# Sink columns copied ahead of the bias transfer, and padded value copies one step later, in a windowed-attention stage

## The chip, the cores and the metric

The kernel runs on one core of one Trainium2 chip. Its time is device microseconds (us) of one execution; lower is better. Five engines work from queues of their own, each strictly in the order in which the program lists its instructions: PE (TensorE: matrix products, with PEld for its weight loads), DVE (VectorE), ACT (ScalarE), POOL (GpSimd) and SP (SyncE, which here only issues DMA transfers). An instruction that waits for another engine or for a transfer holds everything behind it on its engine.

## What is computed

One step of a two-layer encoder for 1024 prompt frames and 32 sample frames, 1056 columns in all, at width 1024. Layer 0 is an mLSTM mixer with a feed-forward block. Layer 1 is attention in a sliding window with a feed-forward block, and only that attention is touched by the change. All heads use one shared pair of keys and values; each query sees its own chunk of 64 frames and the two chunks before it; a distance bias is added, and each head has a learned "sink", a score that takes part in the maximum and in the sum but has no value row:

```
s  = einsum('bcqhgd,bckhd->bchgqk', q, k) * HEAD_DIM ** -0.5 + bias
sk = sinks.reshape(N_KV_HEADS, GROUP)[:, :, None, None]
mx = maximum(max(s, -1), sk)
p  = exp(s - mx)
p  = p / (sum(p, -1) + exp(sk - mx))
o  = einsum('bchgqk,bckhd->bcqhgd', p, v)
x  = layer_norm(alpha * x + o @ w_out)
```

16 query heads share 2 key and value heads of size 64.

## The kernel before

All dense products run on PE as three matmuls for one (high times high, high times low, low times high), since operands are split in a rounded high part and a rest. A weight unit (`wr`, 512 KB) is loaded by SP at line 168, cast to its high part `wh` by ACT or POOL (lines 243 and 245), and the rest `wl` is formed by POOL or DVE (line 247). The helper `gemm` at lines 416 to 418 issues the matmuls and after each triple calls `wv.tick`, which moves a hand-written clock of "model microseconds" forward; generators launched on that clock (`wv.launch`) emit their instructions when their pause has run out. So the order in each queue is fixed when the program is written: dense matmuls with pieces of attention woven in between.

The frames are processed in three column groups (0 to 383, 384 to 767, 768 to 1055), and attention in nine tiles b: eight of 128 prompt frames, and b = 8 for the sample. Four pairs of query tiles `jp`, each of two tiles j, run over group 0 first, then over groups 1 and 2. A "visit" is one `jp` over the tiles of group 0, or over those of groups 1 and 2; the item (j, b) is one query tile on one frame tile. An item goes through these steps of `attention`:

- `scores`: PE forms the products into `psS` (line 1830); DVE adds bias and sink and takes the minimum in one instruction (line 1836, `s<-psS,bt`). At the first item of a visit, the bias of a coming visit is loaded by `load_bias`.
- `soft`: ACT takes exponentials (line 1851).
- `scale`: DVE takes reciprocals (line 1861), POOL multiplies (line 1864; for the first tile b = 0 and for the sample DVE does it, line 1868).
- `turn`: PE transposes the weights into a bank `T` (line 1889), ACT and DVE split them in `hi` and `lo` (lines 1893 and 1894).
- `values`: for odd j, PE multiplies with the values `VR` or with the padded values `VZ` into `O` (line 1918). It is emitted for tile b only once `ast["v"] > b`.
- `place`: ACT and DVE write the result to `act` (lines 1932 and 1936).

The bias tile `bt` holds two rows of 194 columns for each partition: 192 columns of distance bias from a DMA transfer (line 1720, issued by SP), and a sink column at each end of a row, written by two POOL copies (line 1724). There are three buffers of it, and nine loads: two at the start, and one at each of the visits 0 to 6. The sample's tile `sb` has its sink column at one end only (lines 1729 and 1732), one buffer and four loads.

The value tiles come from `v_turn`: for every tile c PE transposes a part of `vT` (line 1785), and `v_parts` splits it into `VR` with ACT and DVE (lines 1712 and 1713). Then `pad_values` copies one half of the partitions of tile c into one or two places of `VZ`, a POOL cast (line 1775). Three generators do this, for groups 0, 1 and 2, launched with pauses of 1.5, 5.0 and 2.5 model us, and 0.8 between tiles; group 0's also clears `VZ` (line 1781). `attention` begins 4.0 model us after its launch. Just before it, `k_spread` issues its DMA transfers of keys on SP (lines 1655 to 1659).

Of the kernel before, what the change touches and what calls it, by code (L numbers as in the profile page):

```python
# [30 lines left out]
WK = 3 * LC  # L31
# [259 lines left out]
def kernel(ctx: ExitStack, tc: tile.TileContext, A, O):  # L291
    nc = tc.nc
# [13 lines left out]
    def new(p, tag, shape, dt=F32, bufs=1):  # L306
        uid[0] += 1
        return p.tile(list(shape), dt, name=f"{tag}_{uid[0]}", tag=tag, bufs=bufs)
# [20 lines left out]
    for j in range(PAIRS):  # L329
        U_Q.append(add("wqk", 2 * j))  # L330
        U_K.append(add("wqk", 2 * j + 1))
        v = ("wv", 2 * j - 2) if j else ("wvg", 0)
# [1376 lines left out]
    def v_parts(c, src, L):  # L1709

        src = src.rearrange("p (g d) -> p g d", g=2)
        nc.scalar.copy(VR[:L, c, :, 0, :], src)
        nc.vector.tensor_sub(VR[:L, c, :, 1, :], src, VR[:L, c, :, 0, :].bitcast(F32))
# [3 lines left out]
    def load_bias(jp):  # L1717

        bt = B[jp] = new(pb, "bt", [P, 2, WK + 2], bufs=3)
        nc.sync.dma_start(bt[:, :, 1 : WK + 1], A["bias"][:, 2 * jp : 2 * jp + 2, :])  # L1720
        for h in range(2):
            r = slice(64 * h, 64 * h + 64)
            sink = nsink[r, 4 * jp + h : 4 * jp + 4 : 2]
            nc.gpsimd.tensor_copy(bt[r, :, 0 : WK + 2 : WK + 1], sink.unsqueeze(2).broadcast_to([64, 2, 2]))

    def load_sample_bias(jp):

        sb = SB[jp] = new(pb, "sb", [2 * DEC, 2, P + DEC + 1])
        nc.sync.dma_start(sb[:, :, 1:], A["sbias"][:, 2 * jp : 2 * jp + 2, :])
        for h in range(2):  # L1730
            r = slice(DEC * h, DEC * h + DEC)
            nc.gpsimd.tensor_copy(sb[r, :, 0], nsink[r, 4 * jp + h : 4 * jp + 4 : 2])

    load_bias(0)
    load_bias(1)
    load_sample_bias(0)
    def keys_values(g):
        if g == 2:
# [33 lines left out]
    def pad_values(i, c, g2):  # L1772

        r = slice(64 * i, 64 * i + 64)
        nc.gpsimd.tensor_copy(VZ[i][r, c - 1 + i], VR[r, c, g2].rearrange("p a d -> p (a d)").bitcast(F32))

    def v_turn(group, pause):
        yield pause
        if not group:
            for i in range(2):  # L1780
                nc.gpsimd.memset(VZ[i][64 * (1 - i) : 64 * (2 - i)].bitcast(F32), 0.0)
        for c, c0, L, g, off in CH:
            if g == group:
                pt = new(psb, "T", [P, 512], bufs=2)
                nc.tensor.transpose(pt[:L, :P], vT[g][:, off : off + L], ident[:])
                v_parts(c, pt[:L, :P], L)
                for i in range(2):
                    if 1 - i <= c < 8 - i:
                        pad_values(i, c, 0)
                ast["v"] = c + 1  # L1790
                yield 0.8

    ast = {"ready": 0, "scored": 0, "placed": 0, "v": 0, "visit": -1}

# [6 lines left out]
    def attention(gap):  # L1801
# [11 lines left out]
        def scores(j, b):  # L1813
            _, t0, R, g, off = CH[b]
            jp = j // 2
            if j % 2 == 0 and b in (0, 3):
                ast["visit"] += 1
                if ast["visit"] < 7:
                    load_bias((ast["visit"] + 1) % 4)
            s = S[j, b] = {}  # L1820
            q, g2, ps = Q[j, g], j // 4, psS[j % 2]
            bias = SB[jp] if b == 8 else B[jp]
            p = s["p"] = new(pb2, "s", [P, 2 * WK + 4], bufs=5)
            st = s["st"] = new(pb2, "st", [P, 3, 2], bufs=6)
            n = DEC if b == 8 else LC
            rows = 2 * n
            for c, at, _, nk, k0, _ in parts(b):
                lhs = q[:, 2 * (off + n * c) : 2 * (off + n * c) + rows]
                for i, k in enumerate((KH[g2], KL[g2])):
                    nc.tensor.matmul(ps[:rows, at : at + nk], lhs, k[:, k0 : k0 + nk], start=i == 0, stop=i == 1)  # L1830
            for c, src, at, nk, _, w in parts(b):
                first = b != 0 and c == 0
                cols = slice(at - first, at + nk + (not first))
                sc = slice(src - first, src + nk + (not first))
                bc = slice(w - first, w + nk + (not first))
                nc.vector.tensor_tensor_reduce(
                    p[:rows, cols], ps[:rows, sc], bias[:rows, j % 2, bc], 1.0, 3e38,
                    op0=ALU.add, op1=ALU.min, accum_out=st[:rows, 0, c : c + 1],
                )
            if b == 8 and j % 2 and jp < 3:  # L1840
                load_sample_bias(jp + 1)
            ast["scored"] += 1
# [111 lines left out]
    for t in spread:  # L1954
        wv.drain(t)
    wv.launch(v_turn(0, 1.5))
    wv.launch(v_turn(1, 5.0))
    task = wv.launch(attention(GAP_A))
    ast["ready"] = 4
    keys_values(2)  # L1960
    wv.launch(v_turn(2, 2.5))
    for t in spread:
        wv.drain(t)
# [182 lines left out]
```

## Time and profile before

| | |
|---|---|
| median of 3 runs | 2208.6 us (2207.87 to 2209.03) |
| the profiled execution, its own time | 2208.45 us |
| its span in the profile | 2206.7 us |
| mean granted TensorE clock | 0.995 of full speed |
| busy DVE, ACT, POOL | 1447.5, 986.7, 976.6 us |
| HBM traffic over the span | 129 GB/s |

Times within the span are counted from its start. The attention items run from about 1210 to 1421 us. A row of the timeline gives start, duration, engine, line, operation, what is written and read and with what shape, and in brackets how long the engine stood idle before it and who let it go. A row of the waits gives the total, the number of times and the longest. A row of the windows gives the length of the stretch, the busy time of each engine with its number of instructions, then PEclk (the granted TensorE clock, 1.00 is full speed), the DMA share and GB/s.

### The profile page before, as it was taken

The page shows a single profiled execution, that of the slowest core. Times are in us where ns is not written, and L with a number is a line of the kernel's source. Part 1 is how long each engine was busy: PE and PEld are TensorE (multiplying, and loading weights), DVE is VectorE, ACT ScalarE, POOL GpSimd, SP SyncE. Part 2 cuts the span into 40 slices and gives each one's busy share as a digit, 9 for nine tenths or more (in the row PEclk, how much of TensorE's full clock was granted, in tenths as well). Part 3 has the DMA queues.
Part 4 walks back from the last instruction along what each step waited for, and adds up shares of the span by engine and source line. Part 5 has one row for each costly group of instructions (what it writes and reads, how often), then busy time and mean ns, then how long its engine had stood idle before and what let it go on. Part 6 is the DMA issues. An engine that isn't in the chain of part 4 may idle for free.

```text
span 2206.7 us, 43768 instructions
## 1 busy us (share of the span) xinstructions
PE 2169.5 (98%) x16982; PEld 2141.5 (97%) x16982; DVE 1447.5 (66%) x2822; ACT 986.7 (45%) x2224; POOL 976.6 (44%) x987
## 2 busy tenths in 40 slices
PE   9999999999999999999999899999999999999997
PEld 9999999999999999999999889899999999999997
DVE  4465576787656655566668777788666666466657
ACT  4443455465444444322235676756444444332125
POOL 2544310004655555544526656600666555554441
PEclk9999999999999999999999999999999999999999
DMA  5221212212443343697515221411344434397712
GB/s 170 78 62 57 58 40 87 89 39 79 156 151 137 142 156 137 234 333 231 180 65 147 87 73 55 133 62 40 119 155 156 146 132 152 137 345 252 246 57 80
DMA packets 166192, 289.97 MB, mean 131 GB/s; under 512 B 16416, under 2 KB 121944, under 8 KB 165984
## 3 DMA queue, kind: packets, MB, share of 16 engines
q1 hardware_dynamic: 161632, 282.84, 38.4%
q10 hardware_dynamic: 4352, 4.33, 0.6%
q8 instruction: 134, 2.20, 0.4%
q14 instruction: 74, 0.61, 0.1%
HBM read 202.35 MB, written 82.94 MB: 129 GB/s over the span
## 4 chain that ended last, share of the span: by engine, by line
PE 84%; DVE 7%; ACT 4%; DMA 3%; issue 2%; POOL 0%; SPq 0%; ACTq 0%; DVEq 0%; POOLq 0%
PE d L416 10%; PE d L418 10%; PE d L417 10%; PE A L416 9%; PE A L417 9%; PE A L418 9%; PE B L416 7%; PE B L417 7%; PE B L418 7%; DMA sx<-hs_t 1%; PE O L1918 1%; ACT act L519 1%; PE psS L1830 1%; DMA sx<-hs_x 1%; PE T L1889 1%
## 5 line engine op out<-in xcount | busy, mean ns | idle before, releaser
L247 POOL TENSOR_TENSOR wl_s<-wr,wh_s 128x512 fp32r<-128x512 f32 x224 | 304.1, 1366 | 237.1 <-ACT wh_s L245 163.6
L416 PE MATMUL d<-sx,wh 128*128 128x264 f32 (+2 forms) x1040 | 333.2, 320 | 1.2 <-DVE act L1680 1.2
L247 POOL TENSOR_TENSOR wl_a<-wr,wh_a 128x512 fp32r<-128x512 f32 x112 | 153.2, 1370 | 402.0 <-ACT wh_a L245 397.5
L418 PE MATMUL d<-sx,wl 128*128 128x264 f32 (+2 forms) x1040 | 317.3, 305 | 1.0 <-POOL wl L247 1.0
L417 PE MATMUL d<-sx,wh 128*128 128x264 f32 (+2 forms) x1040 | 317.3, 305 | 1.1 <-DVE sx L531 1.1
L416 PE MATMUL A<-sx,wh_s 128*128 128x264 f32 x896 | 254.5, 284 | 0.0
L417 PE MATMUL A<-sx,wh_s 128*128 128x264 f32 x896 | 254.2, 284 | 0.0
L418 PE MATMUL A<-sx,wl_s 128*128 128x264 f32 x896 | 254.0, 283 | 0.0
L245 ACT CAST wh_s<-wr 128x512 fp32r<-128x512 f32 x224 | 135.7, 617 | 192.1 <-DVE wr L197 102.4
L416 PEld LDWEIGHTS d<-sx,wh 128*128 128x128 f32 x1040 | 197.3, 190 | 4.4 <-DVE act L1680 1.4
L417 PEld LDWEIGHTS d<-sx,wh 128*128 128x128 f32 x1040 | 197.5, 190 | 2.5 <-DVE sx L531 1.3
L418 PEld LDWEIGHTS d<-sx,wl 128*128 128x128 f32 x1040 | 196.8, 189 | 1.8 <-POOL wl L247 1.5
L416 PE MATMUL d<-sx,ex 128*128 128x264 f32 x624 | 180.7, 290 | 0.1
L418 PE MATMUL d<-sx,ex 128*128 128x264 f32 x624 | 177.0, 284 | 0.7 <-DVE ex L247 0.7
L417 PE MATMUL d<-sx,ex 128*128 128x264 f32 x624 | 177.2, 284 | 0.0
L418 PEld LDWEIGHTS A<-sx,wl_s 128*128 128x128 f32 x896 | 168.8, 188 | 0.0
L416 PEld LDWEIGHTS A<-sx,wh_s 128*128 128x128 f32 x896 | 168.4, 188 | 0.1
L417 PEld LDWEIGHTS A<-sx,wh_s 128*128 128x128 f32 x896 | 168.4, 188 | 0.0
L1346 POOL TENSOR_TENSOR z<-z 128x528 fp32r<-128x528 f32 x76 | 103.2, 1358 | 127.8 <-ACT z L1345 114.4
L247 POOL TENSOR_TENSOR wl<-wr,wh 128x512 fp32r<-128x512 f32 (+2 forms) x84 | 109.6, 1309 | 74.6 <-ACT wh L245 71.9
L416 PE MATMUL A<-ex,wh_s 128*128 128x264 f32 x448 | 127.5, 285 | 0.0
L417 PE MATMUL A<-ex,wh_s 128*128 128x264 f32 x448 | 127.1, 284 | 0.0
(378 smaller groups left out, 7211.2 us busy)
## 6 DMA issues: line engine op xcount, KB each, us to landing
wr<-in_gu SPq DMA_DIRECT2D x92, 512.0 KB, 4.6
hs_x<-z SPq DMA_DIRECT2D x72, 528.0 KB, 3.0
hs_t<-z SPq DMA_DIRECT2D x64, 528.0 KB, 2.8
sx<-hs_x SPq DMA_DIRECT2D x112, 264.0 KB, 5.9
sx<-hs_t SPq DMA_DIRECT2D x64, 264.0 KB, 6.4
ex<-hs_t SPq DMA_DIRECT2D x64, 264.0 KB, 6.7
wr<-in_dn SPq DMA_DIRECT2D x32, 512.0 KB, 3.9
ex<-hs_x SPq DMA_DIRECT2D x32, 264.0 KB, 5.0
```

The costliest lines, as they stand in the source:

```text
L245: self.nc.scalar.copy(hi, r)
L247: eng.tensor_sub(lo, r, hi.bitcast(F32))
L416: nc.tensor.matmul(out, ah, bh, start=start and k == 0, stop=False, **kw)
L417: nc.tensor.matmul(out, ah, bl, start=False, stop=False, **kw)
L418: nc.tensor.matmul(out, al, bh, start=False, stop=stop and k == last, **kw)
L519: nc.scalar.activation(z, z, AF.Identity, scale=gk, bias=bk)
L1346: eng.tensor_sub(lo.bitcast(F32R), buf(s), hi)
L1830: nc.tensor.matmul(ps[:rows, at : at + nk], lhs, k[:, k0 : k0 + nk], start=i == 0, stop=i == 1)
L1889: nc.tensor.transpose(pt[:nk, t, :rows], p[:rows, at : at + nk], ident[:rows, :rows])
L1918: nc.tensor.matmul(out, v[:nk], x, start=i == 0, stop=i == len(todo) - 1)
```

## The change

In `load_bias` and `load_sample_bias` the POOL copies of the sinks stand ahead of the DMA that brings the bias. In `v_turn` the padded copies of tile c are no longer emitted with that tile but two pauses later, just ahead of the transpose of tile c + 2; a last one follows 1.2 model us after the second-last. `ast["v"]`, the count of value tiles that are made, moves with them.

```diff
     def load_bias(jp):
         bt = B[jp] = new(pb, "bt", [P, 2, WK + 2], bufs=3)
-        nc.sync.dma_start(bt[:, :, 1 : WK + 1], A["bias"][:, 2 * jp : 2 * jp + 2, :])
         for h in range(2):
             r = slice(64 * h, 64 * h + 64)
             sink = nsink[r, 4 * jp + h : 4 * jp + 4 : 2]
             nc.gpsimd.tensor_copy(bt[r, :, 0 : WK + 2 : WK + 1], sink.unsqueeze(2).broadcast_to([64, 2, 2]))
+        nc.sync.dma_start(bt[:, :, 1 : WK + 1], A["bias"][:, 2 * jp : 2 * jp + 2, :])
 
     def load_sample_bias(jp):
         sb = SB[jp] = new(pb, "sb", [2 * DEC, 2, P + DEC + 1])
-        nc.sync.dma_start(sb[:, :, 1:], A["sbias"][:, 2 * jp : 2 * jp + 2, :])
         for h in range(2):
             r = slice(DEC * h, DEC * h + DEC)
             nc.gpsimd.tensor_copy(sb[r, :, 0], nsink[r, 4 * jp + h : 4 * jp + 4 : 2])
+        nc.sync.dma_start(sb[:, :, 1:], A["sbias"][:, 2 * jp : 2 * jp + 2, :])
...
     def v_turn(group, pause):
+        def pad(c):
+            for i in range(2):
+                if 1 - i <= c < 8 - i:
+                    pad_values(i, c, 0)
+            ast["v"] = c + 1
+
+        ready = []
         yield pause
...
                 v_parts(c, pt[:L, :P], L)
-                for i in range(2):
-                    if 1 - i <= c < 8 - i:
-                        pad_values(i, c, 0)
-                ast["v"] = c + 1
                 yield 0.8
+                if ready:
+                    pad(ready.pop())
+                ready.append(c)
+        yield 1.2
+        pad(ready.pop())
```

## The prediction

> **What bounds the kernel now.** I read the busy line of the page first, then PE's waits, then the POOL queue around the longest of them, then the chain of waits through it, and last the windows for the clock.
>
> ```profile
> span 2206.7 us, 43768 instructions
> PE 2169.5 (98%) x16982; PEld 2141.5 (97%) x16982; DVE 1447.5 (66%) x2822; ACT 986.7 (45%) x2224; POOL 976.6 (44%) x987
> ...
> PE T L1889 <- POOL s L1864: 6.3, 2, 5.1
> PE O L1918 <- DVE act L1936: 3.9, 4, 2.3
> ...
> POOL bt L1724 <- DMA bt<-in_bias: 25.4, 7, 8.9
> POOL VZ L1775 <- DVE VR L1713: 7.1, 1, 7.1
> ```
>
> PE sets the end: it stands idle for 2206.7 - 2169.5 = 37.2 us of the span. Shortening DVE, ACT or POOL is worth only what it takes from those 37.2 us or from stretches in which PE runs at a lower clock. The largest single wait, 5.1 us, is for a POOL multiplication (the `scale` step). POOL itself waits 25.4 us in seven places for bias transfers before it may copy the sinks. The question is how much of 25.4 lies under 5.1.
>
> ```profile
> 1211.43 0.62 POOL L1775 CAST VZ<-VR 64x128 fp32r<-64x128 f32 x2
> 1220.91 0.41 POOL L1724 COPY bt<-nsink 64x4 f32<-64x4 f32 x2 [8.86 <-DMA bt<-in_bias]
> 1221.39 0.61 POOL L243 CAST wh<-wr 128x512 fp32r<-128x512 f32 x1
> 1222.08 1.26 POOL L247 TENSOR_TENSOR wl<-wr,wh 128x512 fp32r<-128x512 f32 x1
> 1223.28 1.28 POOL L1775 CAST VZ<-VR 64x128 fp32r<-64x128 f32 x4
> 1224.64 0.82 POOL L1864 TENSOR_TENSOR s<-s,st 128x384 f32<-128x384 f32 x1
> ...
> 1225.52 0.90 PE L1889 MATMUL T<-ident,s 128*128 128x128 f32 x3 [5.05 <-POOL s L1864]
> ...
> 1216.36 0.15 DVE L1861 RECIPROCAL st<-st 128x2 f32<-128x2 f32 x1
> ...
> 1217.71 0.59 SPq L1720 DMA_DIRECT2D bt<-in_bias  x1
> ...
> 1212.05 8.84 issue
> ```
>
> POOL is done at 1212.05 and then stands until 1220.91, since SP reached this bias only at 1217.71 and it landed about 3.2 us later. Behind the copies stood a weight split, four padded copies and the multiplication that PE wanted. Its last input was the reciprocal of 1216.36. The chain of waits shows the same hole as 8.84 us of "issue". So PE's 5.05 us are a queueing effect: the multiplication was ready at 1216.5 and ran at 1224.64.
>
> ```profile
> 1220.50:1225.50 5.00, 0.00 (x0) 0.00 (x0) 0.45 (x4) 0.30 (x2) 4.19 (x10) 0.68 0.20 50
> 1225.50:1229.30 3.80, 3.78 (x15) 3.36 (x15) 1.34 (x7) 1.47 (x6) 3.60 (x6) 0.52 0.05 5
> 1229.30:1235.00 5.70, 5.70 (x40) 5.49 (x40) 3.84 (x14) 4.12 (x14) 2.66 (x6) 1.00 0.38 126
> 1430.00:2206.70 776.70, 762.81 (x6232) 759.57 (x6230) 510.94 (x700) 316.30 (x565) 337.89 (x256) 0.99 0.44 149
> ```
>
> The wait has a second price. For 3.80 us after it PE is busy, but at a granted clock of 0.52, so (1 - 0.52) x 3.80 = 1.82 us of work are lost. The last row shows why a gain here lasts: after 1430 PE is busy 762.81 of 776.70 us, so nothing later holds the end in place.
>
> **The sinks.** Nothing is added or removed: 18 copies for `bt`, 8 for `sb`, and 13 transfers all stay. Only the order of two queues against each other changes. POOL no longer waits for a transfer; SP's bias transfer waits for the copies instead, if the two are held to overlap, as the 25.4 us say that they are. At 1212.05 POOL goes on with copies 0.41, cast 0.61, split 1.26 and, were the padded copies still here, 1.28: done by about 1215.7. Then it waits for the reciprocal and multiplies from 1216.5 to 1217.3.
>
> ```profile
> 1220.13 0.34 PE L418 MATMUL d<-sx,wl 128*128 128x384 f32 x1
> ...
> 1221.36 0.23 DVE L1836 CUSTOM_DVE_ANT_0 s<-psS,bt 128x65 f32<-128x65 f32 x1 [1.04 <-POOL bt L1724]
> ...
> 1216.49 0.33 PE L1785 MATMUL T<-ident,act 128*128 128x128 f32 x1 [0.41 <-DVE VR L1713]
> 1218.58 0.38 PE L1889 MATMUL T<-ident,s 128*64 128x128 f32 x2 [0.79 <-DVE lo L1894]
> ```
>
> PE comes to this transpose at 1220.13 + 0.34 = 1220.47. The margin is 3.1 us, so the whole 5.05 us should go, and with it the slow clock, 1.82 us.
>
> What is late next is DVE's first use of this bias. It already waited to 1221.36 and now waits for the landing alone. Its split of PE's transposed tile stands behind that, so DVE reaches it at about 1221.8; PE has its second bank and a `values` product ready until then. In the 8.5 us before the stall PE lost 0.41 + 0.79 us to DVE; in the 5.7 us after it, none (5.70 of 5.70). I charge half of the 1.2 us, **0.6 us**, for a resumed stage with no pause in which DVE catches up.
>
> ```profile
> 1169.95 1.17 POOL L1724 COPY bt<-nsink 64x4 f32<-64x4 f32 x4 [4.17 <-DMA bt<-in_bias]
> ...
> 1205.21 0.40 PE L417 MATMUL d<-sx,wh 128*128 128x288 f32 x1 [1.05 <-DVE sx L531]
> 1207.42 0.40 PE L416 MATMUL d<-sx,wh 128*128 128x288 f32 x1 [1.17 <-DVE act L1680]
> 1208.50 0.36 PE L1785 MATMUL T<-ident,act 128*128 128x128 f32 x1 [0.42 <-DVE VR L1713]
> ...
> 1208.51 0.95 POOL L1775 CAST VZ<-VR 64x128 fp32r<-64x128 f32 x3 [7.14 <-DVE VR L1713]
> ```
>
> At the other six places nobody on PE waits for POOL's copies, so those waits vanish at a gain of nothing. One of them, 4.17 us, stands ahead of the stage. What POOL then does earlier meets DVE's normalisation work earlier. Bounds: PE's gaps at 1205 to 1208.5, 1.05, 1.17 and 0.42 us, are all behind DVE, so a gain of up to 2.64 us; a loss of 1 us if DVE is held at a worse moment. I take nothing: POOL's work changes its place, not its amount.
>
> **SP behind the copies.** SP now stands still until POOL has copied, and everything queued on SP stands with it. The longest new hold is at the seventh load:
>
> ```profile
> 1274.97 0.43 SPq L1720 DMA_DIRECT2D bt<-in_bias  x1
> 1281.12 4.29 SPq L1227 DMA_DIRECT2D act<-scrx  x2
> ...
> 1279.57 0.42 POOL L1724 COPY bt<-nsink 64x4 f32<-64x4 f32 x2
> 1280.07 1.01 POOL L447 TENSOR_TENSOR sx<-act,sx 128x384 fp32r<-128x384 f32 x1
> ```
>
> SP would issue at 1280.0 instead of 1274.97. The next transfer on SP, at 1281.12, starts as the POOL row of 1280.07 ends, so it is not later. The bias itself is used only a visit on. At no other load does POOL stand further behind SP. The sample's copies show no wait for a transfer in the trace, so their swap is worth nothing either way.
>
> **The padded copies.** 14 casts of about 0.29 us move back in POOL's queue, past a weight split and partly past the multiplications.
>
> ```profile
> L1775 POOL CAST VZ<-VR x28: 282/288/327, 1208.5 to 1351.4; 64x128 fp32r<-64x128 f32 x28
> L1918 PE MATMUL O<-hi,VZ x56: 277/281/415, 1235.2 to 1418.6; 128*128 128x256 f32 x56
> ```
>
> They are first read at 1235.2, 26 us after the first tiles are copied, so being later costs nothing. The later `ast["v"]` reaches 3 at 5.1 model us (1.5 + 3 x 0.8 + 1.2), while the first `values` comes after 4.0 and some seven pauses of 0.46, so PE's order stays. What it gives: the 7.1 us wait at 1208.51 no longer holds the first weight split, which can run up to 2 us earlier, and with it SP's next weights and the bias behind them, at most 1.3 us. And 1.28 us of casts leave the way of the multiplication. With the first part done, neither is on PE's path: nothing. Alone, it would be worth some 2 to 3 us.
>
> **Sum.** -5.05 - 1.82 + 0.6 = -6.27 us. From the profiled execution's own 2208.45 us (span 2206.7 and 1.75 around it) to 2202.2; from the median, 0.15 higher, to **2202.3 us**.
>
> **A rule that speaks against it.** DVE slows beside POOL here:
>
> ```profile
> L511 DVE TENSOR_TENSOR act<-act,z x60: 695/703/1781, 420.4 to 2191.5; 128x528 f32<-128x528 f32 x60
> ```
>
> The same instruction takes 0.70 us or up to 1.78. The Trainium skill, SBUF — State Buffer, section "SBUF: two separate sides", says that DVE and GpSimd share one pair of ports, locked for a whole instruction. The trace agrees with 1.78 against 0.70. By that rule a split and a multiplication brought forward, 1.26 + 0.82 us, could hold DVE 2.1 us in place of my 0.6, and the sum would be -4.8 us; by DVE's waits of the rows above, which I follow, it stays -6.27.
>
> **Rivals.**
>
> *The wait moves (to DVE or the bias landing).* For: SP still issues the bias behind a row of key transfers, and DVE still needs it. Against: DVE waited only 1.04 us for it and PE has 3 us of other work. If PE keeps 2 us of the stall and the low clock as well:
>
> ```profile
> 1289.79 0.36 PE L1918 MATMUL O<-hi,VR 128*128 128x256 f32 x1 [2.28 <-DVE act L1936]
> ...
> 1290.00:1300.00 10.00, 9.86 (x67) 9.68 (x67) 7.91 (x32) 6.62 (x20) 7.93 (x9) 0.83 0.32 98
> ```
>
> Here, behind a wait of only 2.28 us (the row of 1289.79), the clock averaged 0.83, a loss of 1.7 us in ten. The gain is then 6.87 - 2 - 1.7 = 3.2 us: **2205.4**. The Trainium skill, TensorE: Matmul & The Clock Gate, Part 1, ties the lower clock to an idle window of about 3.4 us; by that rule alone this rival would keep its 1.7 us. The row does not agree.
>
> *More than the stall goes.* If POOL's earlier start also takes the 2.64 us of gaps around 1205 to 1208: 2208.6 - 6.3 - 2.6 = **2199.7**.
>
> *It doesn't do what it says.* If the copies wait for something else as long, such as readers of the old buffer: **2208.6**. Against: the third buffer is new at this load.
>
> *Slower: POOL's freed work holds DVE.* Place: the six other loads, where POOL stood still and DVE ran alone. Price: a split of 1.26 and a multiplication of 0.82, 2.1 us a load, 12.6 in all; were all of it to reach PE, 2202.3 + 12.6 = **2214.9**. It decides from 6.27 / 6 = 1.05 us a load.
>
> ```profile
> 1150.00:1430.00 280.00, 263.09 (x1842) 250.61 (x1841) 212.07 (x700) 187.36 (x572) 182.62 (x227) 0.98 0.33 98
> ```
>
> Against: POOL's work is no more than before, and DVE is idle for 68 of these 280 us.
>
> **How the numbers follow.** A measurement of this kernel tells about 0.2%, 4.4 us, from no change. Chances: the forecast 0.62 (own range 2199.5 to 2204.2), more 0.10, the moved wait 0.14, no effect 0.06, slower 0.08. So faster 0.72, same 0.20, slower 0.08. The range runs from 2198.0 (the larger gain with 1.7 us of clock more) to 2207.5, which takes in the moved wait and leaves out no effect and slower.
>
> **What would show it.** Right: no wait of POOL for a bias transfer; the multiplication at about 1217; PE's transpose behind it without a gap, and PEclk 1.00 in the 8 us after; SP's bias transfers each just behind POOL's copies. Wrong: a new PE wait of over 2 us in the next 15 us, behind DVE `lo` or the bias; PE's idle after 1230 grown by several us; a weight load on SP held behind a bias transfer.

## The result and the profile after

The changed kernel takes 2203.88 us in the median of 15 runs (2201.61 to 2205.52), the kernel before 2209.2 us in 15 runs (2206.7 to 2211.24): 5.3 us less, ratio 0.9975 with a 95% interval of 0.9967 to 0.9983. The profiled execution took 2202.15 us, its span is 2200.4 us. In the changed kernel the lines have moved: the copies of the sinks are line 1723, the bias transfer line 1724, the multiplication of `scale` line 1872, the transposes of `turn` line 1897. The order of PE's instructions is the same as before; on POOL only the padded copies stand at other places.

The page of the changed kernel, its span and the first busy line:

```profile
span 2200.4 us, 43777 instructions
PE 2167.1 (98%) x16982; PEld 2138.2 (97%) x16982; DVE 1446.3 (66%) x2822; ACT 986.9 (45%) x2224; POOL 977.8 (44%) x987
```

PE is idle for 33.3 us where it was 37.2, and its busy time is 2.4 us shorter, though it does the same work: fewer matmuls ran at a low clock (mean granted clock 0.997, before 0.995). What PE waits for between 1150 and 1430 us (total, times, longest), then what SP waits for there:

```profile
PE O L1926 <- DVE act L1944: 3.9, 4, 2.3
PE d L417 <- DVE sx L531: 1.8, 1, 1.8
PE T L1897 <- POOL s L1872: 1.2, 1, 1.2
PE d L416 <- DVE act L1680: 1.2, 1, 1.2
PE T L1897 <- DVE lo L1902: 0.8, 1, 0.8
...
SPq L1724 <- POOL bt L1723: 14.6, 7, 5.0
```

The wait of 5.1 us for POOL's multiplication is gone (the 1.2 us that are left are a later one, of 1.21 us before). POOL no longer waits for a bias transfer; SP now waits for POOL's copies in its place, 14.6 us in seven places, and none of it appears among PE's waits. One wait has grown: PE for DVE's `sx` of line 531, from 1.05 to 1.8 us.

POOL's queue of the changed kernel around the old stall, and PE's transpose that had stood 5.05 us:

```profile
1211.09 0.41 POOL L1723 COPY bt<-nsink 64x4 f32<-64x4 f32 x2
1211.57 0.61 POOL L243 CAST wh<-wr 128x512 fp32r<-128x512 f32 x1
1212.26 1.28 POOL L247 TENSOR_TENSOR wl<-wr,wh 128x512 fp32r<-128x512 f32 x1
1213.49 0.64 POOL L1775 CAST VZ<-VR 64x128 fp32r<-64x128 f32 x2
1219.17 0.83 POOL L1872 TENSOR_TENSOR s<-s,st 128x384 f32<-128x384 f32 x1 [5.04 <-ACT s L1859]
...
1222.81 0.49 PE L1897 MATMUL T<-ident,s 128*128 128x128 f32 x3
...
1222.80:1230.80 8.00, 8.00 (x56) 7.54 (x55) 5.64 (x26) 6.24 (x25) 7.31 (x16) 1.00 0.32 95
```

The copies carry no bracket: POOL does not stand before them. It now stands 5.04 us before the multiplication, for ACT, because it is early and its operand is not made yet. The multiplication runs at 1219.17 and not at about 1217, since the scores that it works on come later from PE (below); it ends at 1220.0, PE takes it at 1222.81 without a wait, and in the eight us after that (the row of windows) PE is busy throughout at PEclk 1.00, where it had 3.80 us at 0.52.

Yet the stage comes to that point later than before. Measured from PE's mean product near 1152.8 us, which is the same instruction in both, the first value transpose begins 50.6 us later before the change and 51.3 us later after it:

```profile
1152.78 0.61 PE L477 MATMUL ln<-z,onesm 128*128 128x264 f32 x2
...
1203.37 0.27 PE L1785 MATMUL T<-ident,act 128*128 128x128 f32 x1
```
```profile
1152.80 0.60 PE L477 MATMUL ln<-z,onesm 128*128 128x264 f32 x2
...
1204.08 0.27 PE L1792 MATMUL T<-ident,act 128*128 128x128 f32 x1
...
1206.71 0.40 PE L417 MATMUL d<-sx,wh 128*128 128x288 f32 x1 [1.82 <-DVE sx L531]
```

The first two rows are of the kernel before, the others of the changed one. From the transpose to the end of PE's wait for `sx` another 0.8 us are lost (1206.71 beside 1205.21). These two losses, and the parts of the change that they belong to, are what the experiments are for.

### The profile page after: what moved, and what is told of

Read it like the earlier page. It is cut to its first block, busy times and chain, and to the rows that moved or that the text cites. A ratio compares the mean times of both kernels' runs of the same rounds, so it can differ in the third digit from the quotient of the medians.

```text
span 2200.4 us, 43777 instructions
## 1 busy us (share of the span) xinstructions
PE 2167.1 (98%) x16982; PEld 2138.2 (97%) x16982; DVE 1446.3 (66%) x2822; ACT 986.9 (45%) x2224; POOL 977.8 (44%) x987
## 4 chain that ended last, share of the span: by engine, by line
PE 86%; DVE 6%; ACT 3%; DMA 3%; issue 1%; POOL 1%; SPq 0%; ACTq 0%; POOLq 0%; DVEq 0%
PE d L416 10%; PE d L418 10%; PE d L417 10%; PE A L416 9%; PE A L417 9%; PE A L418 9%; PE B L416 7%; PE B L417 7%; PE B L418 7%; PE O L1926 1%; PE psS L1838 1%; DMA sx<-hs_t 1%; PE T L1897 1%; ACT act L519 1%; DMA sx<-hs_x 1%
```

## The experiments

**Theory Q:** the 5 us were a multiplication standing in POOL's queue behind copies that waited for a transfer; the swap inside the visits removes this. The swap of the two loads ahead of the stage only costs: POOL starts its weight splits earlier, beside DVE's normalisation. The padded copies give nothing beside the swap. **Rivals:** the padded copies carry part of the gain; the early loss is chance; the hold of SP costs something.

Eight runs, timed in two sets, the first four on one chip and the last four on another, each beside the kernel before: 2209.04 us in the first set (26 runs), 2208.15 us in the second (24 runs). "Resampled" stands for a 95% interval of a difference of medians, from drawing both sets of runs again and again.

| kernel | us, median | ratio to before, 95% interval |
|---|---|---|
| sinks first in all loads, padded copies as before | 2203.31 | 0.9973 (0.9964 to 0.9983) |
| padded copies alone | 2206.64 | 0.9988 (0.9979 to 0.9996) |
| sinks first in the visits' loads alone | 2201.79 | 0.9969 (0.9957 to 0.9980) |
| sinks first in the loads ahead of the stage alone | 2209.85 | 1.0003 (0.9994 to 1.0012) |
| the changed kernel again | 2204.34 | 0.9981 (0.9972 to 0.9990) |
| the visits' loads alone again | 2201.61 | 0.9971 (0.9961 to 0.9981) |
| the visits' loads and the padded copies | 2201.25 | 0.9971 (0.9961 to 0.9982) |
| bias first, one copy for each sink column | 2202.71 | 0.9974 (0.9964 to 0.9984) |

**Sinks alone.** `load_bias` and `load_sample_bias` as changed, `v_turn` as before.

```diff
         for h in range(2):
...
+        nc.sync.dma_start(bt[:, :, 1 : WK + 1], A["bias"][:, 2 * jp : 2 * jp + 2, :])
...
     def v_turn(group, pause):
                 v_parts(c, pt[:L, :P], L)
                 for i in range(2):
                     if 1 - i <= c < 8 - i:
                         pad_values(i, c, 0)
```

> Sinks ahead of the bias in all loads; the padded copies as before. Theory Q (the 5 us were POOL's multiplication standing behind copies that waited for a transfer, and the padded copies only cost): PE's wait for POOL's s before T is 0 (5.05 before), no PEclk dip behind it, PE's wait for DVE sx at 1205 is 1.1 and not 1.8 us, because the weight split still stands behind the padded copies; time 0 to 2 us under the changed kernel. Rival P (the padded copies carry part of the gain): a stall of 1 to 3 us stays and the time lies 1 to 3 us over the changed kernel.

PE had no wait for the multiplication at this transpose, and its wait for `sx` fell back to 1.06 us:

```profile
1205.65 0.40 PE L417 MATMUL d<-sx,wh 128*128 128x288 f32 x1 [1.06 <-DVE sx L531]
...
1221.50:1229.50 8.00, 8.00 (x56) 7.51 (x55) 5.63 (x27) 6.24 (x25) 7.60 (x13) 1.00 0.44 119
```

The eight us behind the old stall ran at PEclk 1.00. The time, 2203.31, is that of the changed kernel within the noise, as Q said. The swap alone carries the gain; rival P falls.

**Padded copies alone.** The diff of `v_turn`, with both loads as before.

> Only the padded copies one step later; bias ahead of the sinks as before. Theory Q: POOL still waits 25 us for the bias, PE still stalls at the same transpose, 3 to 4 us instead of 5.05, since four padded casts (1.28 us) leave the way of the multiplication; PE's wait for DVE sx at 1205 grows from 1.05 towards 1.8 us since the weight split now runs beside it; time within 2 us of before. Rival P: the stall falls below 2 us, gain over 3 us.

POOL still stood for the bias, longer at this place since it got there earlier, and PE's stall shrank but did not go. POOL's row and PE's row:

```profile
1218.90 0.41 POOL L1724 COPY bt<-nsink 64x4 f32<-64x4 f32 x2 [9.92 <-DMA bt<-in_bias]
...
1222.89 0.55 PE L1897 MATMUL T<-ident,s 128*128 128x128 f32 x3 [1.41 <-POOL s L1872]
```

A second wait for the multiplication, 1.37 us, came 11 us later. The 1.41 us are less than the 3 to 4 expected, since PE too arrived later there (behind the longer wait for `sx`, 1.56 us, and 6.2 us at a clock of 0.50). The gain is 2.4 us, the "2 to 3 us" that the prediction gives this part alone. Of the expectation, the size of the stall was wrong and the wait for `sx` right; a stall under 2 us is what the rival gave. The gain of 2.4 us lies between the 2 us of the one and the 3 us of the other, and its interval, 0.9 to 4.6 us, does not decide between them.

**The visits' loads alone.** The two loads ahead of the stage keep the transfer first, as do the sample's; so this kernel differs from the sinks alone by the sample's loads too, which no run changes by themselves.

```diff
-    def load_bias(jp):
+    def load_bias(jp, first=False):
...
+        if first:
+            nc.sync.dma_start(bt[:, :, 1 : WK + 1], A["bias"][:, 2 * jp : 2 * jp + 2, :])
         for h in range(2):
...
+        if not first:
+            nc.sync.dma_start(bt[:, :, 1 : WK + 1], A["bias"][:, 2 * jp : 2 * jp + 2, :])
...
-    load_bias(0)
-    load_bias(1)
+    load_bias(0, True)
+    load_bias(1, True)
```

> Sinks ahead of the bias only in the seven loads inside the visits; the two loads ahead of the stage, the sample's load and the padded copies as before. Theory Q with an early cost (POOL's first copies 3.6 us earlier put its splits beside DVE's normalisation): everything up to the stall as in the kernel before, so PE's first value transpose at 1203.4 (1204.1 in the changed kernel), then no stall: gain 6.5 to 7.5 us, the best of these four. Rival (the early loss is chance or belongs to the loop's loads): first value transpose at 1204 again, gain no better than 5.5 us.

> The loop's loads alone once more, for the interval. Theory with an early cost: 1 to 2 us under the changed kernel, 6.5 to 7.5 us under before; value transposes begin 50.4 us after the first mean product of 1152.8, against 51.3 us in the changed kernel. Rival (no early cost): equal to the changed kernel within 0.5 us.

Both runs gave 7.3 and 6.5 us under before, and in both the first value transpose began 50.4 us after the mean product, beside 50.6 us in the kernel before. Beside the changed kernel in the second set, the medians are 2201.61 (9 runs, 2200.16 to 2202.32) and 2204.34 (11 runs, 2200.97 to 2205.0): 2.7 us where 1 to 2 us were expected, and 0.9 to 3.5 us when the runs are resampled. So the changed kernel gives back some 1 to 3 us of what its swap gains, and this version beats both kernels. Beside the sinks alone, in the first set, it is 1.5 us faster, -0.9 to 3.1 us resampled, which does not tell the two apart.

**The loads ahead of the stage alone.** The same edit with the two cases exchanged.

> Sinks ahead of the bias only in the two loads ahead of the stage; all else as before. Theory Q with an early cost: POOL's splits of 1171 start 3 us earlier, DVE's instructions of 1168 to 1172 take twice as long, PE waits 0.3 us for DVE z before a mean product, first value transpose 0.5 to 0.8 us later; the stall of 5 us stays; time 0.5 to 2.5 us over before. Rival (no early cost): the same as before within 0.4 us, markers unchanged.

DVE and POOL in the kernel with only this part, 1168 to 1172 us, and PE's wait; POOL's `oh` and `VR` splits of line 247 stand where POOL had waited for a transfer before:

```profile
1168.10 1.51 DVE L658 TENSOR_TENSOR z<-z,act 128x528 f32<-128x528 f32 x1
1169.64 1.40 DVE L660 TENSOR_TENSOR z<-z 128x264 f32<-128x264 f32 x1
1171.48 0.99 DVE L505 SCALAR_TENSOR_TENSOR z<-z 128x264 f32<-128x264 f32 x1
...
1167.74 1.30 POOL L247 TENSOR_TENSOR oh<-wr,oh 128x512 fp32r<-128x512 f32 x1
1169.00 3.18 POOL L247 TENSOR_TENSOR VR<-wr,VR 128x512 fp32r<-128x512 f32 x2
...
1171.10 0.71 PE L477 MATMUL ln<-z,onesm 128*128 128x264 f32 x2 [0.30 <-DVE z L660]
```

The same DVE instructions in the kernel with the visits' loads alone, where POOL still waits there:

```profile
1168.47 0.71 DVE L658 TENSOR_TENSOR z<-z,act 128x528 f32<-128x528 f32 x1
1169.22 0.43 DVE L660 TENSOR_TENSOR z<-z 128x264 f32<-128x264 f32 x1
1170.09 0.43 DVE L505 SCALAR_TENSOR_TENSOR z<-z 128x264 f32<-128x264 f32 x1
```

DVE needs 3.90 us instead of 1.57 for these three, and PE, which needs the second of them, waits 0.30 us. At this product PE is 0.5 us later than with the visits' loads alone (19.0 us after the mean product near 1152.8 beside 18.6); the few tenths that follow were not traced. The first value transpose begins 51.2 us after the mean product, with the stall of 5.54 us behind it untouched. The ten traces of this study split into two groups: 51.2 to 51.3 us in all four in which the early loads were swapped (the changed kernel twice, sinks alone, this one), 50.4 to 50.6 us in all six others. That the loss is chance is out. In the time this kernel is 0.8 us over before, which the interval does not tell from nothing.

The Trainium skill, SBUF — State Buffer, section "SBUF: two separate sides", says that a DVE instruction with two SBUF inputs and a GpSimd one that reads SBUF cannot run at once. The trace agrees: DVE's second instruction took 0.43 us alone and 1.40 us beside a POOL split of some 1.6 us (3.18 us for two).

**The changed kernel again.**

> The changed kernel once more, beside the others on one chip. Theory: 5 to 6 us under before; first PE wait for DVE sx 1.5 to 1.9 us; no stall at the transpose; the length of the low-clock stretches behind the short waits at 1207 and at 1285 differs from the first trace of the same kernel.

4 us under before, not 5 to 6 (ratio interval 0.9972 to 0.9990, beside 0.9967 to 0.9983 the first time). The wait for `sx` was 1.84 us, no stall stood at the transpose. The last sentence of this expectation was wrong: the clock behind the short waits was the same as in the first trace of the kernel (0.70 over 11 us, 1.00 over ten).

**The visits' loads and the padded copies.** The edit of the visits' loads with the diff of `v_turn`.

> Loop's loads with the sinks first and the padded copies one step later; the loads ahead of the stage as before. Theory: the padded copies add nothing once the stall is gone, and cost what the weight split beside DVE's sx costs: PE's wait there 1.5 to 1.8 us, time 0 to 1 us over the loop's loads alone. Rival (they help by freeing POOL): 0.5 us or more under the loop's loads alone.

PE's wait for `sx` is 1.56 us:

```profile
1206.33 0.41 PE L417 MATMUL d<-sx,wh 128*128 128x288 f32 x1 [1.56 <-DVE sx L531]
```

The time, 2201.25, is 0.4 us under the visits' loads alone, with -1.1 to 1.4 us when the runs are resampled: the padded copies neither help nor cost by an amount that these runs can tell, neither the 0 to 1 us expected nor the rival's 0.5 us. Against the changed kernel, from which it differs only in the loads ahead of the stage and the sample's, it is 3.1 us faster, 0.8 to 3.7 us resampled: here the time itself shows that those swaps cost something, though the traces place only 0.9 us of it ahead of the value transposes (51.3 beside 50.4 us) and 0.3 us at the wait for `sx` (1.84 beside 1.56). The wait for `sx` does follow the padded copies: 1.56 to 1.84 us in all four traces with later padded copies, 1.02 to 1.06 in five of the six without, and 1.39 in the sixth. Its cause stands in two rows of the changed kernel, DVE's `sx` beside the weight split that ran behind the padded copies before:

```profile
1204.83 1.27 POOL L247 TENSOR_TENSOR wl<-wr,wh 128x512 fp32r<-128x512 f32 x1
...
1205.43 1.23 DVE L531 TENSOR_TENSOR sx<-act,sx 128x528 fp32r<-128x528 f32 x1
```

The same instruction took 0.71 us before.

Later on the padded copies give about as much back. These are POOL's multiplication and DVE's last value split, first with the visits' loads alone (second run), then with the padded copies as well:

```profile
1217.80 0.83 POOL L1867 TENSOR_TENSOR s<-s,st 128x384 f32<-128x384 f32 x1
1217.93 0.84 DVE L1713 TENSOR_TENSOR VR<-cv,VR 128x128 fp32r<-128x128 f32 x1
```
```profile
1217.80 0.83 POOL L1875 TENSOR_TENSOR s<-s,st 128x384 f32<-128x384 f32 x1 [4.08 <-ACT s L1862]
1218.46 0.32 DVE L1713 TENSOR_TENSOR VR<-cv,VR 128x128 fp32r<-128x128 f32 x1
```

In the kernel before it took 0.28 us, as POOL stood still. In all four traces without the stall and with the padded copies at their old place it takes 0.84 us, and PE's wait for `lo` behind it is 1.34 to 1.35 us; in the three with later padded copies it takes 0.32 us and the wait is 0.82 to 0.83 us. So the padded copies cost PE 0.5 us at `sx` and spare it 0.5 us at `lo`.

**One copy for each sink column.** Bias first, as before; in the visits' loads four copies of two columns instead of two of four.

```diff
-            nc.gpsimd.tensor_copy(bt[r, :, 0 : WK + 2 : WK + 1], sink.unsqueeze(2).broadcast_to([64, 2, 2]))
+            if early:
+                nc.gpsimd.tensor_copy(bt[r, :, 0 : WK + 2 : WK + 1], sink.unsqueeze(2).broadcast_to([64, 2, 2]))
+            else:
+                for e in (0, WK + 1):
+                    nc.gpsimd.tensor_copy(bt[r, :, e], sink)
```

> Order and padded copies as before, bias transfer first; in the loop's loads each sink column is copied by an instruction of its own (four copies for two), so that no copy's address range spans the columns that the transfer writes. Theory (POOL waited for a transfer that writes other columns, because one copy with two far columns is held to overlap it): POOL's seven loop waits for the bias vanish without any change of order, SP does not wait for POOL, time like the loop's loads alone, 6 to 7.5 us under before. Rival (the whole tile is held): POOL waits as before, time like before.

Of POOL's waits for the bias only the one ahead of the stage is left:

```profile
POOL bt L1725 <- DMA bt<-in_bias: 4.0, 1, 4.0
```

PE has no stall at the transpose, and SP waits for no copy. So POOL had waited for columns that the transfer does not write: one copy that reaches from the first column to the last was held to overlap the transfer between them. It is the range of columns that counts, and not a flat range of addresses, as the expectation had it: each new copy writes one column of both rows, and so still reaches in addresses across the transfer's first row. (The sample's copies, of one column in two rows, had no wait from the start.) The gain is 5.4 us, under the 6 to 7.5 us expected; the time, 2202.71, is not told apart from that of the visits' loads alone (1.1 us more, -1.6 to 2.8 when resampled). As this kernel is no faster without SP's hold, which is 13.7 us with the visits' loads alone, that hold costs nothing that can be measured.

## Why the prediction was right, and which terms were off

The forecast was 2202.3 us, a gain of 6.3; measured are 5.3 us.

PE runs the same instructions in the same order in both kernels, so the start of one instruction in both traces tells what has been gained or lost up to it. Three more rows of the changed kernel, then one of the kernel before:

```profile
1221.11 0.38 PE L1897 MATMUL T<-ident,s 128*64 128x128 f32 x2 [0.82 <-DVE lo L1902]
...
1226.73 0.49 PE L1897 MATMUL T<-ident,s 128*128 128x128 f32 x3
...
1284.95 0.36 PE L1926 MATMUL O<-hi,VR 128*128 128x256 f32 x1 [2.29 <-DVE act L1944]
```
```profile
1231.16 0.49 PE L1889 MATMUL T<-ident,s 128*128 128x128 f32 x3
```

The changed kernel is 1.5 us late behind the wait for `sx`, and 2.5 us late at the transpose ahead of the old stall (1221.11 - 1218.58); the added 1.0 us fell where its clock was 0.70 and before 0.84. At the stalled transpose it is 2.7 us early (1225.52 - 1222.81), at the next transposes 4.4 us (1231.16 - 1226.73), at the wait of 2.28 us 4.8 us (1289.79 - 1284.95), at the end 6.3 us (the spans); most of the last step is the clock behind that wait, 0.83 before and 1.00 after. So the two main terms brought 5.2 and 1.7 us, while 2.5 us of loss ahead of them and 1.9 us of gain behind them were not in the sum. That this one execution gained 6.30 us beside a forecast of 6.27 is luck; the median gained 5.3.

- **The stall, -5.05 us.** Right. POOL passes its copies without a wait, PE's transpose has no gap. Sinks alone and separate copies show it, each by a different edit. From the transpose ahead of the stall to the stalled one it was 6.94 us before (1218.58 to 1225.52) and is 1.70 to 1.72 us in all seven traces without the stall.
- **The low clock behind it, -1.82 us.** Right at this place: PEclk is 1.00 for eight us in the changed kernel and with the sinks alone. The next step, 5.64 us before (1225.52 to 1231.16), is 3.92 to 3.95 us in the same seven traces: 1.7 us.
- **DVE, +0.6 us.** Not there in the changed kernel: PE loses nothing behind the old stall, and 0.82 us to `lo` at 1221.11 where 0.79 stood before. With the swap inside the visits and the padded copies as before it is there, 0.55 us at that wait, since DVE's value split then falls beside POOL's multiplication (0.84 for 0.28 us). The prediction named this under "a rule that speaks against it"; it did not see that the padded copies would move the two apart.
- **The loads ahead of the stage, taken as nothing.** This is the step that was mis-sized. The prediction named the mechanism ("DVE is held at a worse moment") and bounded it at 1 us, then took zero because POOL's work only changes its place. Place was what counted: 0.7 us in the trace up to the value transposes. The same holds for the later padded copies, whose earlier weight split I counted as a possible gain; it fell beside DVE's `sx`, and with the swap the wait grew by 0.8 us. With 1.5 us for both and without the 0.6 the sum would have been 6.87 - 1.5 = 5.4 us. That this is near the median's 5.3 proves little, as the clock behind short waits alone moves a trace by more than the difference.
- **SP behind the copies.** Right: the longest hold is 5.0 us, as worked out, and costs nothing that can be measured.
- **Padded copies.** Right that they add nothing beside the swap, by two parts of 0.5 us that cancel and that the prediction did not have; the 2.4 us that they gained alone fit its 2 to 3 us.
- **Rivals.** The wait did not move to DVE or the landing. The slower rival's mechanism is real at one of its six places, the loads ahead of the stage, and at two it did not name (`sx` and `lo`), each below the 1.05 us a load from which it decides. "More than the stall goes" had the sign of the early gaps wrong: of 1.05, 1.17 and 0.42 us, the first grew to 1.82, the second stayed and the third went, 2.99 us for 2.64.

## What to carry to other kernels

When an in-order engine waits for a transfer before a small copy, look at what stands behind that copy in its queue and who needs it; the wait costs as much as that work comes late, and another order, or copies that stay within their own columns, removes it. Where a split of POOL's slows DVE's work beside it (here 0.43 us to 1.40), a wait of POOL's may be shielding DVE: before removing all copies of a wait, ask at each place what will run there instead, and remove only those that something is late for. Differences of this size want one part alone and a marker in the trace: the median of the kernel before differed by 0.9 us between the two sets, at over twenty runs each.

## What was not expected of the hardware

The low clock behind short waits does not come out the same from trace to trace. Windows of 11 us behind PE's two waits at 1205 to 1209 us, for the kernel with the early loads alone, the changed kernel, and the visits' loads alone (first run); the clock is the third figure from the end:

```profile
1207.37:1218.37 11.00, 9.38 (x68) 8.37 (x69) 7.97 (x53) 6.70 (x32) 3.28 (x7) 1.00 0.48 125
```
```profile
1208.92:1219.92 11.00, 10.58 (x56) 9.73 (x57) 6.29 (x43) 4.92 (x23) 4.41 (x10) 0.70 0.57 148
```
```profile
1209.29:1220.29 11.00, 10.96 (x51) 10.37 (x51) 5.71 (x38) 4.25 (x20) 6.31 (x14) 0.56 0.48 126
```

Two waits of 1.0 to 1.8 us and 1.2 us were followed by a loss of nothing, of 3.3 us (0.30 x 11) or of 4.8 us (0.44 x 11). The second run of the visits' loads alone had 0.69 here. The same wait of 2.28 us near 1285 us was followed by ten us at a clock of 1.00 in the changed kernel, both times, and at 0.69 with the sinks alone:

```profile
1284.95:1294.95 10.00, 9.86 (x77) 9.62 (x78) 8.64 (x34) 7.81 (x25) 8.09 (x10) 1.00 0.33 105
```
```profile
1283.71:1293.71 10.00, 10.00 (x58) 9.76 (x59) 6.87 (x26) 6.76 (x21) 7.55 (x9) 0.69 0.31 104
```

That is 3 us at one wait, as much as half of what the change gains. The two traces of the visits' loads alone, one kernel, had 0.83 and 1.00 here: they are 3.0 us apart when this wait ends (1286.61 and 1283.64) and 4.2 us at the end (spans of 2203.4 and 2199.2). But 2.1 us of that are there at the mean product already (1154.53 and 1152.46), long before. So the clock is a part of the 2 to 6 us by which the runs of each kernel spread; how large a part was not tested. The Trainium skill, TensorE: Matmul & The Clock Gate, Part 1, ties the low clock to an idle window of about 3.4 us that runs on its own; a start that differs between runs fits that, but low clock behind waits of 1.0 to 2.3 us does not. So how long a low clock follows a short wait could not be read off one trace. Behind the stall of over 5 us it came in both traces that have one: 0.52 for 3.80 us before, and 0.50 for 4.60 us with the early loads alone.
